# Layer 0: the product behind the MLP's norm takes six feature tiles beside the norm instead of twelve

## The chip, the cores and the metric

The kernel runs on one core of a Trainium2 chip. The metric is device time in microseconds (us) of one execution, as the median of several runs. A core has a matrix engine (TensorE, PE in the profile; its weight loads are listed apart as PEld), a vector engine (VectorE, DVE), a scalar engine (ScalarE, ACT), a general engine (GpSimd, POOL) and a queue engine (SyncE, SP) that here only issues DMA transfers. Each engine takes its instructions in the order in which the program lists them.

## The reference

Two layers over 256 tokens of 2048 features. Each layer normalises the residual `x`, scales and shifts it with values made from a conditioning vector, runs two groups of attention, adds the gated result, normalises again and runs a dense MLP:

```
mod = cond @ w_ada[l] + b_ada[l]
sh_a, sc_a, g_a, sh_m, sc_m, g_m = split(mod, 6)
...
h = _rmsnorm(x) * (1.0 + sc_m) + sh_m
y = square(relu(h @ w_mlp_in[l])) @ w_mlp_out[l]
x = x + g_m * y
```

`w_mlp_in` is 2048 x 8192. The change concerns the first quarter of its columns in layer 0 (2048 features, 16 tiles of 128 columns, called feature tiles here), the norm ahead of that product and the work in the same queues. All arithmetic is float32; products run on two parts of each operand (below).

## The kernel before, in words

Every product is made from two-part numbers. A weight matrix arrives as float32 in a tile `raw` (SyncE issues the DMA, L173); ACT rounds it to a first part `hi` (L154) and DVE takes the rest, `lo = raw - hi` (L157). Activations have the same two parts. A product is then hi x hi, hi x lo and lo x hi. Seven `raw` buffers and four each of `hi` and `lo` are there, so that weights are at most a few pieces ahead of the matmuls.

There are two ways to multiply one weight tile with the 256 tokens. In `mac` (L197, L200, L201) it takes three matmuls with 256 columns each, and all three land in one half of a bank of PSUM. In the wide form the two parts of the activation stand side by side as 512 columns: one matmul of 512 columns (L220 in `wides`, L287 in `wide_by_k`) makes both hi products, into the two halves of a bank, and one of 256 columns (L223, L284) adds the lo product. A wide tile needs a bank of its own, and the halves have to be added later (`joined`: a copy on ACT, L1440, and an addition on DVE, L1441).

`norm_then_by_k` makes the second norm of a layer and multiplies as it goes. It turns `x` by 128 features, and for each of eight steps p it makes two k tiles of `h` (two times 128 features): DVE scales (`ht`, L715), ACT adds the shift and rounds to the first part (L718), DVE makes the second part (L723). Then the weights of the two k tiles are prepared and multiplied into all open banks. In layer 0 it keeps 12 feature tiles in six banks, two a bank, by `by_k` and `mac`; each step p takes two pieces of weights of 128 x 1536. In layer 1 it keeps six feature tiles in six banks by `wide_by_k`, with one such piece a step. `first_block` then (layer 0) makes the relu and square of the 12 tiles, the other four tiles with `wides`, and the product with the first quarter of `w_mlp_out` (`rows`, L314 to L317).

Between all this runs the conditioning work. `mod` needs 192 pieces of `w_ada` of 1 MB: `ada_load` issues one DMA into a `raw` buffer, and `ada_sums` multiplies and sums it on DVE (L383), an instruction on 128 x 2048 elements. Two such sums give two columns of one group of `mod` (L395 or L397). How many are issued is set by a credit: each call of `weights` adds `self.rate`, and a piece is loaded for each full 1.0 (`more_ada`); its sum stands behind a later piece of weights on DVE. `ada_need` loads at once whatever the norm needs and lacks. The pieces of the shift and scale of layer 0's second norm are themselves among those that are still summed while that norm runs: step p reads columns 2p and 2p+1.

Of the kernel before, what the change touches and what calls it, by code (L numbers as in the profile page):

```python
# [94 lines left out]
WHOLE = 6  # L95


RATE_A0, RATE_V, RATE_A1, RATE_A2, RATE_K, RATE_K1, RATE_M0 = 1.1, 1.6, 0.6, 0.9, 0.6, 0.3, 1.0
RATE_M3 = 0.75
RATE_S, RATE_R, RATE_E = (0.1, 0.2), (0.8, 0.5), 0.3  # L100
RAWS = 7
# [3 lines left out]
class Trunk:  # L105
# [636 lines left out]
    def norm_then_by_k(self, l, sh, sc, src):  # L742

        nc = self.nc
        end = self.last_mm
        raws = [self.raw(src[0, b], 1536) for b in range(2 - l)]
        parts = [self.part(raws[0], i, 768)[0] for i in range(2)]
        r, rb = self.s("rms"), self.bank("pn")[:, 0]
        x = [self.turned(0, end)]
        self.behind(self.last_square, self.last_turn)  # L750
        root = [self.roots(r, t) for t in range(2)]
        self.spread_one(rb, r, 0, self.last_turned)
        x.append(self.turned(1, self.last_spread, True, self.last_x))
        self.behind(root[1][1], self.last_turn)
        x.append(self.turned(2, self.last_turned, False, root[1][0]))
        act = self.last_turn
        x.append(self.turned(3, self.last_turned, True, root[1][1]))
        x.append(self.turned(4, self.last_turned, False, act))
        act = self.last_turn
        late = [self.turn_in(i, self.last_turned) for i in (5,)]  # L760
        self.spread_one(rb, r, 1, self.last_turned)
        late += [self.turn_in(i, self.last_spread) for i in (6, 7)]
        h, gate, banks = [], None, None
        for p in range(8):
            k = 2 * p
            for g in (sh, sc):
                self.ada_need(l, g, k + 1)
            new, ins = self.modulated(x[p], rb, k, self.mod[l, sh], self.mod[l, sc], gate, act if p == 0 else None)
            gate = None
            h += new  # L770
            if p == 0:
                x += [self.turn_out(ps, False, self.last_h) for ps in late]
                banks = self.open_banks(6)
                gate = ins, self.last_turn
                for i in range(2, 2 * len(raws)):
                    w, ins = self.part(raws[i // 2], i % 2, 768, ins)
                    parts.append(w)
                blocks = [(parts[2 * b : 2 * b + 2], 768) for b in range(len(raws))]
            else:
                order = (self.last_h, ins) if p == 1 else None  # L780
                blocks = self.by_k_weights([src[p, b] for b in range(2 - l)], 6, False, order)
            if l == 0:
                self.by_k(banks, blocks, h, k, NK, 6, apart=p == 0)
            else:
                self.wide_by_k(banks, blocks, h, k, NK)
        return h, banks

    def first_norm_then_by_k(self, acc, src, n, fill, early):
# [96 lines left out]
    def layer(self, l, acc=None):  # L885
# [160 lines left out]

        self.quiet = False
        self.rate = RATE_K1 if l else RATE_K
        h, banks = self.norm_then_by_k(l, 3, 4, io["w_m0"] if l == 0 else io["w_m01"])
        self.kept = {}  # L1050
        if l == 0:
            self.first_block(h, banks)
# [6 lines left out]
    def first_block(self, h, banks):  # L1059

        io = self.io
        hid = []
        self.rate = RATE_M0
        for b in banks:
            hid += self.relu2(b)
        for m in range(12, NK, 2):
            ps = self.wides([io["w_m10"][m + j - 12] for j in range(2)], h)
            hid += self.relu2(self.joined(ps, self.t("sum")))
        left = []
        for c in range(4):  # L1070
            pss = self.rows(io["w_m2"][0, 0], hid, c)
            left.append(pss)
            if c == 1:
                self.keep_left(left)
            elif c > 1:
                self.keep_right(pss, c)

    def last_block(self, h):

        io = self.io  # L1080
        hid, acc = [], {}
        self.rate = RATE_M3
        self.gate(0, 5)
        steps = [lambda: self.read_kept(acc, (1, 2, 3)), lambda: self.read_kept(acc, (4, 5, 6, 7)),
                 lambda: self.add_halves(self.merged(acc))]
        for m in range(0, NK, 2):
            ps = self.wides([io["w_m10"][NK * 3 + m + j - 12] for j in range(2)], h)
            hid += self.relu2(self.joined(ps, self.t("sum")))
            if m > 4 and steps:
                steps.pop(0)()  # L1090
        for c in range(4):
            pss = self.rows(io["w_m2"][0, 3], hid, c, c == 3)
            self.updates(pss, c, True)
            if c == 0:
                self.read_kept(acc, [(t, c) for c in (2, 3) for t in range(2)])
            elif c == 1:
                for t, g in ((0, 2), (1, 2), (0, 3), (1, 3)):
                    self.add_rows(acc[t, g], t, g)
# [19 lines left out]
    def block_by_seven(self, l, fb, h, banks):  # L1118
# [8 lines left out]
        for m in range(plain, NK, 2):  # L1127
            both = self.t("sum")
            for j in range(2):
                src = io["w_m11"][NK * fb + m + j - 6] if l else io["w_m10"][NK * fb + m + j - 12]  # L1130
                ps = self.wides([src], h)[0]
                self.join(ps, both[:, j])
                if len(pairs) > 1:
                    pairs[-2][j]()
            r = self.relu(both)
            parts = self.split(r, "hid")
            hid += parts
            pairs.append(self.seven(io[f"w_ms{l}"][fb, m // 2], parts, r, sums, m == plain, m == NK - 2))
            if end and m == 2:
                self.gate(l, 5)  # L1140
# [508 lines left out]
def _kquarters(w, c=512, per=4):  # L1649
    k = w.shape[0] // P  # L1650
    return np.ascontiguousarray(w.reshape(k // per, per, P, c).transpose(0, 2, 1, 3)).reshape(k // per, P, per * c)
# [11 lines left out]
def _layout(i):  # L1663
    f = {k: np.asarray(v) for k, v in i.items()}
    a = {}
# [19 lines left out]
    for l in range(2):  # L1685
        w = f["w_in"][l]
        first = np.concatenate([w[:, 3072:3840], w[:, :768]], 1)
        if l == 0:
            a["w_a"] = np.stack([_kquarters(np.ascontiguousarray(first[:, 768 * j : 768 * j + 768]), 768, 2) for j in range(2)], 1)
        else:  # L1690
            a["w_a1"] = _kquarters(np.ascontiguousarray(first[:, :768]), 768, 2)[:, None]
            a["w_q1"] = _ktiles(np.ascontiguousarray(first[:, 768:]))
        keep["w_t"].append(_ktiles(np.ascontiguousarray(w[:, 1280:2048])))
        keep["w_d"].append(_kquarters(np.concatenate([w[:, 1024:1280], w[:, 768:1024]], 1)))
# [8 lines left out]
        w = np.concatenate([f["w_o"][l][1024:], f["w_o"][l][:1024]])  # L1703
        keep["w_o"].append(_kcols(w))
        w = f["w_mlp_in"][l]
        if l == 0:
            a["w_m0"] = np.stack([_kquarters(np.ascontiguousarray(w[:, 768 * j : 768 * j + 768]), 768, 2) for j in range(2)], 1)
        else:
            a["w_m01"] = _kquarters(np.ascontiguousarray(w[:, :768]), 768, 2)[:, None]
        a[f"w_m1{l}"] = _ktiles(np.ascontiguousarray(w[:, 1536 - 768 * l :]))  # L1710
        keep["w_m2"].append(np.stack([_kcols(f["w_mlp_out"][l][D * b : D * b + D]) for b in range(NFB)]))
    for l in range(2):
        a[f"w_ms{l}"] = np.stack([_kblocks(f["w_mlp_out"][l][D * b : D * b + D, :1024]) for b in range(NFB)])
# [21 lines left out]
```

## Time and profile before

| | us |
|---|---|
| median of 3 runs | 2141.35 (2141.03 to 2141.7) |
| the profiled execution | 2140.8 |
| its span in the profile | 2139.0 |
| first matmul of the product beside layer 0's second norm | 400.11 |
| first matmul of the four later tiles | 469.49 |
| the same two places in layer 1 (six tiles beside the norm) | 1441.09 and 1474.98 |

Times in the trace count from the start of the span. A row of the timeline gives the start of a group of equal instructions, the time from the start of the first to the end of the last, engine, line, operation, output and inputs, the shape and the count. Instructions of one engine overlap by their latency: of DVE's and ACT's rows the step from one start to the next is what the engine needs, and the last row's end is when the result is there. An entry in square brackets is idle time ahead of the row and what ended it.

### The profile page before, as it was taken

What the parts mean: (1) busy time and instruction counts of PE and PEld (TensorE: products, weight loads), DVE (VectorE), ACT (ScalarE), POOL (GpSimd) and SP (SyncE); (2) the same over time, 40 slices, a digit from 0 to 9 for tenths busy, and PEclk for the clock granted to TensorE, in tenths of its full rate; (3) what the DMA queues carried; (4) which work ended last, traced back from release to release, by engine and by line L of the source; (5) the groups of instructions that cost most, each with busy time, mean ns of one, the idle gap of its engine ahead of it and who ended that gap; (6) DMA issues with size and microseconds to landing.
All of it is one profiled execution on the core that took longest, in us unless ns stands there. A gap on an engine that the chain in (4) does not pass through costs nothing.

```text
span 2139.0 us, 29861 instructions
## 1 busy us (share of the span) xinstructions
PE 2112.4 (99%) x11363; PEld 1828.4 (85%) x11363; DVE 1805.1 (84%) x2453; ACT 1262.3 (59%) x1868; POOL 82.4 (4%) x121
## 2 busy tenths in 40 slices
PE   7999999999999999999999999999999999999998
PEld 6899888898888888888889998888888888888886
DVE  8889888989799888879977896789977985885898
ACT  6555663564466566645454576647755665674674
POOL 0000000000000100111000000000010010010010
PEclk9999999999999999999999999999999999999999
DMA  9999898789965965899968777877595687566664
GB/s 397 423 386 340 320 353 350 284 315 408 387 218 189 363 235 212 296 403 381 396 252 302 281 280 255 305 270 246 210 376 221 236 264 243 197 232 215 216 225 145
DMA packets 99264, 621.80 MB, mean 291 GB/s; under 512 B 11504, under 2 KB 11952, under 8 KB 32304
## 3 DMA queue, kind: packets, MB, share of 16 engines
q1 hardware_dynamic: 85536, 586.41, 72.4%
q0 software_dynamic: 12864, 32.28, 6.1%
q8 instruction: 89, 1.46, 0.3%
q10 hardware_dynamic: 720, 1.19, 0.2%
q14 instruction: 55, 0.45, 0.1%
HBM read 595.43 MB, written 21.27 MB: 288 GB/s over the span
## 4 chain that ended last, share of the span: by engine, by line
PE 94%; DVE 2%; DMA 2%; ACT 1%; issue 0%; SPq 0%; ACTq 0%; DVEq 0%
PE ps L220 20%; PE ps L223 10%; PE pr L314 9%; PE pr L315 9%; PE pr L317 9%; PE pp L1273 3%; PE pp L1275 3%; PE pp L1274 3%; PE pk L263 3%; DMA ada<-in_w_ada 2%; PE pk L197 2%; PE pk L201 2%; PE pk L200 2%; PE pk L287 2%; PE pv L299 2%; PE pv L301 2%
## 5 line engine op out<-in xcount | busy, mean ns | idle before, releaser
L154 ACT ACTIVATE hi<-raw 128x1024 fp32r<-128x1024 f32 (+2 forms) x714 | 713.0, 1010 | 499.6 <-PE pr L315 177.4
L157 DVE TENSOR_TENSOR lo<-raw,hi 128x1024 fp32r<-128x1024 f32 (+2 forms) x714 | 813.6, 1161 | 220.9 <-ACT hi L154 95.3
L383 DVE SCALAR_TENSOR_TENSOR ada<-ada,cond 128x2048 f32<-128x2048 f32 x192 | 438.7, 2287 | 13.4 <-DMA ada<-in_w_ada 12.4
L220 PE MATMUL ps<-h,hi 128*128 128x512 f32 x1856 | 441.0, 391 | 0.3 <-DVE sum L1441 0.2
L220 PEld LDWEIGHTS ps<-h,hi 128*128 128x128 f32 x1856 | 344.0, 188 | 75.5 <-DVE sum L1441 5.5
L314 PE MATMUL pr<-hi,hidh 128*128 128x512 f32 x640 | 249.1, 389 | 0.1
L315 PE MATMUL pr<-hi,hidl 128*128 128x512 f32 x640 | 249.0, 389 | 0.0
L223 PEld LDWEIGHTS ps<-h,lo 128*128 128x128 f32 x1856 | 236.4, 191 | 8.1
L223 PE MATMUL ps<-h,lo 128*128 128x256 f32 x1856 | 238.9, 283 | 0.0
L317 PE MATMUL pr<-lo,hidh 128*128 128x512 f32 x640 | 158.7, 389 | 0.0
L314 PEld LDWEIGHTS pr<-hi,hidh 128*128 128x128 f32 x640 | 120.2, 188 | 25.4 <-ACT hi L154 0.5
L317 PEld LDWEIGHTS pr<-lo,hidh 128*128 128x128 f32 x640 | 120.1, 188 | 24.9
L315 PEld LDWEIGHTS pr<-hi,hidl 128*128 128x128 f32 x640 | 120.1, 188 | 24.9
L157 DVE TENSOR_TENSOR lo<-comb,hi 128x1024 fp32r<-128x1024 f32 x90 | 109.9, 1221 | 6.4 <-ACT hi L154 3.4
L154 ACT ACTIVATE hi<-comb 128x1024 fp32r<-128x1024 f32 x90 | 94.7, 1053 | 17.2 <-PE pp L1275 12.2
L197 PE MATMUL pk<-h,hi 128*128 128x256 f32 x320 | 90.4, 285 | 0.2 <-ACT h L718 0.2
L201 PE MATMUL pk<-h,lo 128*128 128x256 f32 x320 | 90.5, 283 | 0.0
L200 PE MATMUL pk<-h,hi 128*128 128x256 f32 x320 | 90.5, 283 | 0.0
L1440 ACT ACTIVATE sum<-ps 128x256 f32<-128x256 f32 x110 | 41.7, 381 | 75.8 <-PE ps L223 74.8
L263 PE MATMUL pk<-hf,w 128*128 128x256 f32 x384 | 83.9, 379 | 0.0
L263 PEld LDWEIGHTS pk<-hf,w 128*128 128x128 f32 x384 | 72.6, 190 | 10.2 <-ACT hf L690 0.4
L1273 PE MATMUL pp<-hi,sh 128*128 128x512 f32 x180 | 70.2, 394 | 0.0
(292 smaller groups left out, 3431.9 us busy)
## 6 DMA issues: line engine op xcount, KB each, us to landing
ada<-in_w_ada SPq DMA_DIRECT2D x192, 1024.0 KB, 7.3
raw<-in_w_m SPq DMA_DIRECT2D x190, 1024.0 KB, 7.0
raw<-in_w_ms SPq DMA_DIRECT2D x48, 1024.0 KB, 5.4
raw<-in_w_o SPq DMA_DIRECT2D x32, 1024.0 KB, 6.3
raw<-in_w_m SPq DMA_DIRECT2D x24, 768.0 KB, 5.8
kept<-part POOLq DMA_DIRECT2D x69, 256.0 KB, 9.9
raw<-in_w_dv SPq DMA_DIRECT2D x16, 1024.0 KB, 5.8
raw<-in_w_t SPq DMA_DIRECT2D x12, 1024.0 KB, 5.3
```

The lines of the kernel that those rows point to most:

```text
L154: ins = self.nc.scalar.activation(hi, v, AF.Copy)
L157: ins = self.nc.vector.tensor_tensor(lo, v, hi.bitcast(F32), ALU.subtract)
L200: mm(ps, hi, x[1], start=False, stop=False, skip_group_check=shared)
L201: self.last_mac = mm(ps, lo, x[0], start=False, stop=last, skip_group_check=shared)
L220: mm(ps.rearrange("p a b -> p (a b)"), part(w, k, 0), x[2], start=k == 0, stop=False)
L223: mm(ps[:, 0], part(w, k, 1), x[0], start=False, stop=k == nk - 1)
L263: self.nc.tensor.matmul(ps, v, whole[k], start=first, stop=last, skip_group_check=True)
L314: mm(ps, xh[:, c], part(i, 0), start=kq == 0 and i == 0, stop=False)
L315: mm(ps, xl[:, c], part(i, 0), start=False, stop=False)
L317: self.last_mm = mm(ps, xh[:, c], part(i, 1), start=False, stop=kq == 3 and i == 3)
L383: ins = nc.vector.scalar_tensor_tensor(w, w, 1.0, self.cond, ALU.mult, ALU.mult, accum_out=acc[:, i : i + 1])
L1273: nc.tensor.matmul(ps, x[0], wh, start=first, stop=False)
```

## The change

Layer 0 now does what layer 1 does. `norm_then_by_k` takes six feature tiles in six banks with `wide_by_k`, and one piece of 128 x 1536 a step; `first_block` joins the six banks by pairs and makes ten later tiles, not four, with `wides`. The weights are laid out to suit. Two rates change: `RATE_K` (the calls in layer 0's second norm) from 0.6 to 1.0, and `RATE_M0` (`first_block`) from 1.0 to 0.85.

```diff
-RATE_A0, RATE_V, RATE_A1, RATE_A2, RATE_K, RATE_K1, RATE_M0 = 1.1, 1.6, 0.6, 0.9, 0.6, 0.3, 1.0
+RATE_A0, RATE_V, RATE_A1, RATE_A2, RATE_K, RATE_K1, RATE_M0 = 1.1, 1.6, 0.6, 0.9, 1.0, 0.3, 0.85
...
-        raws = [self.raw(src[0, b], 1536) for b in range(2 - l)]
+        raws = [self.raw(src[0], 1536)]
...
-                blocks = self.by_k_weights([src[p, b] for b in range(2 - l)], 6, False, order)
-            if l == 0:
-                self.by_k(banks, blocks, h, k, NK, 6, apart=p == 0)
-            else:
-                self.wide_by_k(banks, blocks, h, k, NK)
+                blocks = self.by_k_weights([src[p]], 6, False, order)
+            self.wide_by_k(banks, blocks, h, k, NK)
...
-        for b in banks:
-            hid += self.relu2(b)
-        for m in range(12, NK, 2):
-            ps = self.wides([io["w_m10"][m + j - 12] for j in range(2)], h)
+        plain = len(banks)
+        for m in range(0, plain, 2):
+            hid += self.relu2(self.joined(banks[m : m + 2], self.t("sum")))
+        for m in range(plain, NK, 2):
+            ps = self.wides([io["w_m10"][m + j - 6] for j in range(2)], h)
             hid += self.relu2(self.joined(ps, self.t("sum")))
```

The other lines of the diff only follow the new layout of the weights (indices, names and the arrays made on the host).

What this does to the order of the queues is seen at three places.

**Steps p = 2 to 4 of layer 0's second norm, on DVE.** `lo` is a piece of weights of one k tile, `ada` a conditioning sum, `ht` and `h` the activations; the number at the end of a name tells buffers apart. Before, there were two pieces of weights, four `lo`, to a step:

```order
L157 TENSOR_TENSOR lo_3725<-raw_3722,hi_3724 128x768
L157 TENSOR_TENSOR lo_3729<-raw_3722,hi_3728 128x768
L383 SCALAR_TENSOR_TENSOR ada_3438,macc_82<-ada_3438,cond 128x2048
L157 TENSOR_TENSOR lo_3739<-raw_3736,hi_3738 128x768
L397 TENSOR_TENSOR mod_81<-macc_82,vec 128x2
L157 TENSOR_TENSOR lo_3743<-raw_3736,hi_3742 128x768
L383 SCALAR_TENSOR_TENSOR ada_3734,macc_84<-ada_3734,cond 128x2048
L723 SCALAR_TENSOR_TENSOR h_3820<-ht_3819,mod_81,h_3820 128x256
L723 SCALAR_TENSOR_TENSOR h_3821<-ht_3819,mod_81,h_3821 128x256
```

After the change, from the weights of step 2 to those of step 4:

```order
L157 TENSOR_TENSOR lo_3714<-raw_3711,hi_3713 128x768
L157 TENSOR_TENSOR lo_3718<-raw_3711,hi_3717 128x768
L383 SCALAR_TENSOR_TENSOR ada_3676,macc_84<-ada_3676,cond 128x2048
L715 SCALAR_TENSOR_TENSOR ht_3748<-xT_3585,mod_83,pn_3553 128x256 x2
L157 TENSOR_TENSOR lo_3760<-raw_3757,hi_3759 128x768
L723 SCALAR_TENSOR_TENSOR h_3749<-ht_3748,mod_81,h_3749 128x256
L723 SCALAR_TENSOR_TENSOR h_3750<-ht_3748,mod_81,h_3750 128x256
L157 TENSOR_TENSOR lo_3764<-raw_3757,hi_3763 128x768
L383 SCALAR_TENSOR_TENSOR ada_3722,macc_84<-ada_3722,cond 128x2048
L715 SCALAR_TENSOR_TENSOR ht_3795<-xT_3592,mod_83,pn_3553 128x256
L395 SCALAR_TENSOR_TENSOR mod_83<-macc_84,vec 128x2
L715 SCALAR_TENSOR_TENSOR ht_3795<-xT_3592,mod_83,pn_3553 128x256
```

So one `ada` now stands in each step, ahead of that step's `ht`, where a step has half the `lo` and half the matmuls of before. On ACT, in the same steps after the change (step 3 has `h_3749` and `h_3750`; the four `hi` ahead of them belong to steps 3 and 4):

```order
L154 ACTIVATE hi_3759<-raw_3757 128x768
L154 ACTIVATE hi_3763<-raw_3757 128x768
L154 ACTIVATE hi_3806<-raw_3804 128x768
L154 ACTIVATE hi_3810<-raw_3804 128x768
L718 ACTIVATE h_3749<-ht_3748,mod_81 128x256
L718 ACTIVATE h_3750<-ht_3748,mod_81 128x256
```

**The last step, p = 7, on DVE.** Before, its two `h` stood apart, with one sum of another group between:

```order
L383 SCALAR_TENSOR_TENSOR ada_4165,macc_84<-ada_4165,cond 128x2048
L157 TENSOR_TENSOR lo_4265<-raw_4262,hi_4264 128x768
L395 SCALAR_TENSOR_TENSOR mod_83<-macc_84,vec 128x2
L715 SCALAR_TENSOR_TENSOR ht_4345<-xT_3625,mod_83,pn_3555 128x256
L157 TENSOR_TENSOR lo_4269<-raw_4262,hi_4268 128x768
L383 SCALAR_TENSOR_TENSOR ada_4260,macc_86<-ada_4260,cond 128x2048
L723 SCALAR_TENSOR_TENSOR h_4346<-ht_4345,mod_81,h_4346 128x256
```

After the change, from step 6's `h` to step 7's first:

```order
L723 SCALAR_TENSOR_TENSOR h_3889<-ht_3888,mod_81,h_3889 128x256
L723 SCALAR_TENSOR_TENSOR h_3890<-ht_3888,mod_81,h_3890 128x256
L157 TENSOR_TENSOR lo_3904<-raw_3897,hi_3903 128x768
L383 SCALAR_TENSOR_TENSOR ada_3862,macc_84<-ada_3862,cond 128x2048
L383 SCALAR_TENSOR_TENSOR ada_3908,macc_84<-ada_3908,cond 128x2048
L157 TENSOR_TENSOR lo_3948<-raw_3945,hi_3947 128x768
L395 SCALAR_TENSOR_TENSOR mod_83<-macc_84,vec 128x2
L157 TENSOR_TENSOR lo_3952<-raw_3945,hi_3951 128x768
L715 SCALAR_TENSOR_TENSOR ht_3936<-xT_3623,mod_83,pn_3553 128x256 x2
L157 TENSOR_TENSOR lo_4021<-raw_4018,hi_4020 128x1024
L723 SCALAR_TENSOR_TENSOR h_3937<-ht_3936,mod_81,h_3937 128x256
```

Two sums in a row now stand ahead of step 7. On PE the program after the change puts 14 matmuls of the first later tile between step 6 and step 7 (`ps_4017` is that tile's bank, `pk_3625` a bank of the norm's product); the last five of the 14 and what follows:

```order
L220 MATMUL ps_4017<-h_3797,hi_4024 128x512
L220 MATMUL ps_4017<-h_3842,hi_4024 128x512
L220 MATMUL ps_4017<-h_3843,hi_4024 128x512
L220 MATMUL ps_4017<-h_3889,hi_4024 128x512
L220 MATMUL ps_4017<-h_3890,hi_4024 128x512
L287 MATMUL pk_3625<-h_3937,hi_3947 128x512
```

**Steps 1 to 3 of layer 1's second norm, on DVE.** The code there is untouched, but the credit arrives with another remainder. Before:

```order
L383 SCALAR_TENSOR_TENSOR ada_13111,macc_98<-ada_13111,cond 128x2048
L723 SCALAR_TENSOR_TENSOR h_13374<-ht_13373,mod_93,h_13374 128x256
L397 TENSOR_TENSOR mod_97<-macc_98,vec 128x2
L723 SCALAR_TENSOR_TENSOR h_13375<-ht_13373,mod_93,h_13375 128x256
L157 TENSOR_TENSOR lo_13385<-raw_13382,hi_13384 128x768
L157 TENSOR_TENSOR lo_13389<-raw_13382,hi_13388 128x768
L715 SCALAR_TENSOR_TENSOR ht_13416<-xT_13258,mod_95,pn_13226 128x256 x2
```

After the change:

```order
L383 SCALAR_TENSOR_TENSOR ada_12935,macc_98<-ada_12935,cond 128x2048
L723 SCALAR_TENSOR_TENSOR h_13200<-ht_13199,mod_93,h_13200 128x256
L397 TENSOR_TENSOR mod_97<-macc_98,vec 128x2
L723 SCALAR_TENSOR_TENSOR h_13201<-ht_13199,mod_93,h_13201 128x256
L157 TENSOR_TENSOR lo_13211<-raw_13208,hi_13210 128x768
L157 TENSOR_TENSOR lo_13215<-raw_13208,hi_13214 128x768
L383 SCALAR_TENSOR_TENSOR ada_13173,macc_98<-ada_13173,cond 128x2048
L715 SCALAR_TENSOR_TENSOR ht_13243<-xT_13082,mod_95,pn_13050 128x256 x2
```

A second sum stands ahead of step 3 there; before, the second came between steps 5 and 6. In layer 1's first norm, the other way round, the second sum moves one step later.

More of the change, by code (lines that the diff above doesn't have):

```diff
@@ L1048, in layer @@
         self.rate = RATE_K1 if l else RATE_K
-        h, banks = self.norm_then_by_k(l, 3, 4, io["w_m0"] if l == 0 else io["w_m01"])
+        h, banks = self.norm_then_by_k(l, 3, 4, io[f"w_m0{l}"])
         self.kept = {}
@@ L1086, in last_block @@
         for m in range(0, NK, 2):
-            ps = self.wides([io["w_m10"][NK * 3 + m + j - 12] for j in range(2)], h)
+            ps = self.wides([io["w_m10"][NK * 3 + m + j - 6] for j in range(2)], h)
             hid += self.relu2(self.joined(ps, self.t("sum")))
@@ L1129, in block_by_seven @@
             for j in range(2):
-                src = io["w_m11"][NK * fb + m + j - 6] if l else io["w_m10"][NK * fb + m + j - 12]
+                src = io[f"w_m1{l}"][NK * fb + m + j - 6]
                 ps = self.wides([src], h)[0]
@@ L1690, in _layout @@
         else:
-            a["w_a1"] = _kquarters(np.ascontiguousarray(first[:, :768]), 768, 2)[:, None]
+            a["w_a1"] = _kquarters(np.ascontiguousarray(first[:, :768]), 768, 2)
             a["w_q1"] = _ktiles(np.ascontiguousarray(first[:, 768:]))
@@ L1705, in _layout @@
         w = f["w_mlp_in"][l]
[L1706 to L1710, printed above, removed]
+        a[f"w_m0{l}"] = _kquarters(np.ascontiguousarray(w[:, :768]), 768, 2)
+        a[f"w_m1{l}"] = _ktiles(np.ascontiguousarray(w[:, 768:]))
         keep["w_m2"].append(np.stack([_kcols(f["w_mlp_out"][l][D * b : D * b + D]) for b in range(NFB)]))
```

## The prediction

> **What bounds the kernel now.** I read the page first: the share of each engine, then the chain that ended last.
>
> ```profile
> span 2139.0 us, 29861 instructions
> PE 2112.4 (99%) x11363; PEld 1828.4 (85%) x11363; DVE 1805.1 (84%) x2453; ACT 1262.3 (59%) x1868; POOL 82.4 (4%) x121
> PE 94%; DVE 2%; DMA 2%; ACT 1%; issue 0%; SPq 0%; ACTq 0%; DVEq 0%
> ```
>
> The matmuls are 94% of the chain. Of PE's waits between 400 and 2100 us the longest line is this one (for whom, us in total, times, longest):
>
> ```profile
> PE pp L1273 <- ACT hi L154: 0.9, 1, 0.9
> PE pk L284 <- ACT h L718: 0.5, 2, 0.2
> ```
>
> So PE hardly waits there, and whatever PE gains or loses in one stage reaches the end almost whole. Next I asked for windows over the stage that changes, and over the same stage in layer 1, which already has the form that layer 0 gets.
>
> ```profile
> core 0: us, PE busy (x) PEld busy (x) DVE busy (x) ACT busy (x) POOL busy (x), PEclk, DMA share, GB/s
> 405.00:415.00 10.00, 10.00 (x85) 10.00 (x85) 10.00 (x14) 4.80 (x7) 0.00 (x0) 1.00 0.84 297
> 425.00:435.00 10.00, 10.00 (x86) 10.00 (x85) 9.97 (x14) 4.80 (x8) 0.00 (x0) 1.00 0.95 331
> 1450.00:1460.00 10.00, 10.00 (x58) 8.74 (x57) 10.00 (x19) 6.19 (x12) 0.00 (x0) 1.00 0.91 313
> ```
>
> The point is the fourth column: DVE is full in both stages, at a granted clock of 1.00. PE is served, but with nothing to spare.
>
> **PE's own work.** The timeline gives the pace of the two forms.
>
> ```profile
> 400.11 0.62 PE L197 MATMUL pk<-h,hi 128*128 128x256 f32 x3 [0.24 <-ACT h L718]
> 469.25 0.28 PE L200 MATMUL pk<-h,hi 128*128 128x256 f32 x1
> 469.37 0.28 PE L201 MATMUL pk<-h,lo 128*128 128x256 f32 x1
> 469.49 3.82 PE L220 MATMUL ps<-h,hi 128*128 128x512 f32 x16
> 1441.09 0.62 PE L284 MATMUL pk<-h,lo 128*128 128x256 f32 x3 [0.24 <-ACT h L718]
> 1449.78 1.55 PE L287 MATMUL pk<-h,hi 128*128 128x512 f32 x6
> 1451.17 0.88 PE L284 MATMUL pk<-h,lo 128*128 128x256 f32 x6
> 1453.98 1.55 PE L287 MATMUL pk<-h,hi 128*128 128x512 f32 x6
> 1474.98 3.82 PE L220 MATMUL ps<-h,hi 128*128 128x512 f32 x16
> 1478.64 2.08 PE L223 MATMUL ps<-h,lo 128*128 128x256 f32 x16
> 1480.55 3.82 PE L220 MATMUL ps<-h,hi 128*128 128x512 f32 x16
> ```
>
> Twelve tiles beside the norm take 469.49 - 400.11 = 69.38 us, 0.12 a matmul and 0.36 a tile and k tile. Six wide tiles take 1474.98 - 1441.09 = 33.89: a step (two k tiles) is 1453.98 - 1449.78 = 4.20, or 0.35 a tile and k tile. A later wide tile takes 1480.55 - 1474.98 = 5.57. So PE's work is 69.38 + 4 x 5.57 = 91.66 before and 33.89 + 10 x 5.57 = 89.59 after: **-2.1 us**, if nothing keeps it waiting.
>
> [...] The rows show 120 for 256 columns and 232 (1.39/6) for 512, and I keep 2.1.
>
> **DVE's queue beside the norm.** A step loses half its matmuls and half its `lo`, but each of the eight steps keeps its `ht` and `h`, and the seven sums (`ada`) that this norm itself needs must all come before step 7. I priced the new order from the same instructions in layer 1.
>
> ```profile
> 399.04 0.87 DVE L715 SCALAR_TENSOR_TENSOR ht<-xT,mod,pn 128x256 f32<-128x256 f32 x2
> 1440.01 0.87 DVE L715 SCALAR_TENSOR_TENSOR ht<-xT,mod,pn 128x256 f32<-128x256 f32 x2
> 1446.19 2.29 DVE L383 SCALAR_TENSOR_TENSOR ada<-ada,cond 128x2048 f32<-128x2048 f32 x1
> 1448.41 0.48 DVE L723 SCALAR_TENSOR_TENSOR h<-ht,mod,h 128x256 fp32r<-128x256 f32 x1
> 1448.81 0.15 DVE L397 TENSOR_TENSOR mod<-macc,vec 128x2 f32<-128x2 f32 x1
> 1448.88 0.48 DVE L723 SCALAR_TENSOR_TENSOR h<-ht,mod,h 128x256 fp32r<-128x256 f32 x1
> 1449.27 1.82 DVE L157 TENSOR_TENSOR lo<-raw,hi 128x768 fp32r<-128x768 f32 x2
> 1451.01 0.87 DVE L715 SCALAR_TENSOR_TENSOR ht<-xT,mod,pn 128x256 f32<-128x256 f32 x2
> 1451.79 0.95 DVE L157 TENSOR_TENSOR lo<-raw,hi 128x768 fp32r<-128x768 f32 x1
> 1452.66 0.88 DVE L723 SCALAR_TENSOR_TENSOR h<-ht,mod,h 128x256 fp32r<-128x256 f32 x2
> 1468.62 0.48 DVE L723 SCALAR_TENSOR_TENSOR h<-ht,mod,h 128x256 fp32r<-128x256 f32 x1
> 1470.28 2.38 DVE L157 TENSOR_TENSOR lo<-raw,hi 128x1024 fp32r<-128x1024 f32 x2
> ```
>
> From start to start: two `ht` 0.78, two `h` 0.79, a `lo` of 768 columns 0.87 and of 1024 about 1.15, a sum 2.22, a `mod` 0.07. Layer 0 starts its first `ht` at 399.04 and its first matmul at 400.11; layer 1 at 1440.01 and 1441.09. The two agree to 0.02 and their queues are equal up to the `lo` of step 2, so I put layer 0's new queue on layer 1's clock.
>
> Step 3: layer 1 starts its `ht` at 1451.01. There the new order has a sum first; `ht` starts at 1453.23, one `lo` later `h` starts at 1454.88 and is there at 1455.36. PE wants it at 1453.98: **1.4 late**. From step to step the new queue holds 0.78 + 0.79 + 2 x 0.87 + 2.22 = 5.53, and 5.60 with a `mod`, against PE's 4.20. Steps 4, 5 and 6 add 1.40, 1.33 and 1.40. From step 6's first `h` to step 7's there are two `h`, three `lo` of 768, two sums, a `mod`, two `ht` and a `lo` of 1024: 0.79 + 2.61 + 4.44 + 0.07 + 0.78 + 1.15 = 9.84. PE has step 6 (4.20) and the 14 matmuls drawn forward (14 x 3.66/16 = 3.20): 2.4 late. Sum: 1.4 + 1.4 + 1.3 + 1.4 + 2.4 = **+7.9 us** of waiting for DVE's `h`. While PE waits there nothing else is queued ahead on it; behind it DVE and ACT have the later tiles' weights, at 5.57 a tile with about 3 us of DVE plus a sum, so PE isn't kept there again.
>
> ACT makes a second chain of the same length. In the new order `h` of step n stands behind both `hi` of step n+1, and the second of these needs the buffer that PE frees with the second group of 512 columns of step n-1.
>
> ```profile
> 1451.37 0.85 ACT L154 ACTIVATE hi<-raw 128x768 fp32r<-128x768 f32 x1 [1.25 <-PE pk L287]
> 1452.12 0.89 ACT L718 ACTIVATE h<-ht,mod 128x256 fp32r<-128x256 f32 x2
> ```
>
> The first `hi` starts 0.20 after its group ended (1451.17). The second would start 2.10 + 1.39 + 0.20 = 3.69 after the step, `h`'s first part 0.75 later, 0.5 long, then 0.1 and DVE's 0.48: 5.5 to 5.6 a step again. So shorter sums alone would not shorten the wait.
>
> The joins: 12 more, each about 0.4 on ACT and on DVE, beside ten tiles of 5.57; the rest of the weights are the same bytes. I cost them and `RATE_M0` at nothing; if uncovered, the last join before `rows` would cost some 2 us. The ends for layer 0 are 0 and about 11 us of waits; I take 7.9, since all its terms are rows of the same instructions.
>
> **Layer 1's norms.** The second norm gets a sum ahead of step 3, as above: 1.4 late. Its third sum stands ahead of step 7: today's first `h` there starts at 1468.62, with 2.3 more it is there at 1471.4, and PE (1470.78, now 1.4 later) wants it at 1472.2. So **+1.4** (0 to 2). In the first norm the one wait today goes when the sum moves a step later, **-0.45** (0 to -0.45):
>
> ```profile
> 1122.02 1.67 PE L287 MATMUL pk<-h,hi 128*128 128x512 f32 x6 [0.45 <-DVE h L723]
> ```
>
> **Sum.** -2.1 + 7.9 + 1.4 - 0.45 = +6.8 us. The profiled execution took 2140.8 (its span 2139.0 and 1.8 around it): 2147.6. The median of the runs is 0.55 above that execution: **2148.2 us**.
>
> **Rivals.**
> - *The wait stays hidden (not slower).* Were DVE's `h` always ahead, only -2.1 and -0.45 remain: 2138.8. It turns on the sums per step: DVE has 3.31 us of other work in PE's 4.20, so 0.40 of a sum fits and one doesn't. For it speaks that layer 1 waits nowhere with two sums; against, that layer 0 has seven. 6%.
> - *Half of it.* The lead that DVE has at step 3 (0.84 in layer 1: 1453.14 against 1453.98) is larger in layer 0, or instructions run closer together: 4 us of waits, about 2144.4. 12%.
> - *Transfers become the bound.* A new step moves 0.79 + 1.05 MB in 5.6 us, 328 GB/s, what the stage carries today at a DMA share of 0.95. A buffer freed by step n's `lo` is wanted as step n+3's weights about 6.0 us after the issue:
>
> ```profile
> raw<-in_w_m SPq DMA_DIRECT2D x10, 768.0 KB, 6.0
> ```
>
>   That is the median landing. If landings take 7.5, each of two turns of the seven buffers adds 1.5: 2151. 8%.
> - *Weight loads are the bound (faster).* PEld is 10.00 of 10 in layer 0's stage and 8.74 in layer 1's. If loads set the pace at 0.12 each, two instead of three save 192 x 0.12 = 23 us: 2118. Against it, layer 1 shows 0.35 for two loads and not 0.24. 3%. [...]
>
> **How the numbers follow.** Forecast 71%, with the four rivals 6, 12, 8 and 3. A measurement of this kernel can tell about 0.2%, 4.3 us, from no change. Slower by more: 71 + 8, and a hair of the half case, 0.80. Within: the hidden case and most of the half, 0.17. Faster: 0.03. The range 2143.5 to 2151.5 leaves out the hidden case, the loads, and the ends of the half and the transfer cases, some 18%.
>
> **What would show it.** In the new profile, PE's waits: about 8 us for DVE's `h` at L287 in layer 0, in five pieces ahead of steps 3 to 7, the last the longest; a piece of 1.4 in layer 1's second norm and none in its first. The stretch from 400 to the first `rows` would grow from 91.7 to about 97.5. If the waits end on the DMA of `raw` or on ACT's `hi`, the transfers decide. If PE has none and the stretch is 89.6, the queue count is wrong. If the total is off with these waits as said, the loss or gain is in a stage that I took as unchanged, where the sums have also moved.

## The result and the profile after

| | us |
|---|---|
| before, median of 6 runs beside the changed kernel | 2141.68 (2141.03 to 2143.5) |
| after, median of 6 runs | 2150.22 (2148.95 to 2150.71) |
| ratio | 1.0038, 95% interval 1.0027 to 1.0049 |
| the profiled execution after, and its span | 2150.71, 2148.9 |

The change makes the kernel slower by 8.5 us; the forecast was 2148.2, and the measured median lies inside the forecast's range of 2143.5 to 2151.5. The profiled executions differ by more, 2150.71 - 2140.8 = 9.9 us. The page of the profile after, its span and busy times:

```profile
span 2148.9 us, 29476 instructions
PE 2110.8 (98%) x11171; PEld 1819.8 (85%) x11171; DVE 1806.5 (84%) x2461; ACT 1266.5 (59%) x1876; POOL 82.3 (4%) x121
```

PE has 1.6 us less work and ends 9.9 us later: what was won in matmuls is lost in waits. PE's waits between 400 and 2140 us (for whom, us in total, times, longest) name them:

```profile
PE pk L287 <- DVE h L723: 8.3, 6, 2.1
PE pp L1271 <- ACT hi L154: 3.7, 4, 0.9
...
PE pp L1272 <- DVE lo L157: 0.5, 1, 0.5
```

Five of the six waits for `h` are in layer 0's second norm and one is in layer 1's. PE's timeline of the kernel after shows them, with the rows that bound the stages:

```profile
401.12 0.61 PE L284 MATMUL pk<-h,lo 128*128 128x256 f32 x3 [0.24 <-ACT h L718]
413.29 0.87 PE L284 MATMUL pk<-h,lo 128*128 128x256 f32 x6
415.43 1.66 PE L287 MATMUL pk<-h,hi 128*128 128x512 f32 x6 [1.27 <-DVE h L723]
416.93 0.88 PE L284 MATMUL pk<-h,lo 128*128 128x256 f32 x6
417.64 1.55 PE L287 MATMUL pk<-h,hi 128*128 128x512 f32 x6
419.03 0.87 PE L284 MATMUL pk<-h,lo 128*128 128x256 f32 x6
421.09 1.66 PE L287 MATMUL pk<-h,hi 128*128 128x512 f32 x6 [1.20 <-DVE h L723]
...
436.74 3.36 PE L220 MATMUL ps<-h,hi 128*128 128x512 f32 x14
442.25 1.66 PE L287 MATMUL pk<-h,hi 128*128 128x512 f32 x6 [2.15 <-DVE h L723]
...
498.93 0.40 PE L314 MATMUL pr<-hi,hidh 128*128 128x512 f32 x1
...
1461.57 1.66 PE L287 MATMUL pk<-h,hi 128*128 128x512 f32 x6 [1.28 <-DVE h L723]
```

A step that doesn't wait puts its next group 0.71 after the start of an L284 row (416.93 to 417.64). So the group at 415.43 is 415.43 - 414.00 = 1.43 late, the one at 421.09 is 1.35 late, and the last, 3.20 after 436.74, is 2.31 late. The bracket shows some 0.16 less each time, since the row ahead ends that much behind the place where the next group was due (416.93 + 0.88 = 417.81, against 417.64), and the first group after a wait takes 0.11 longer (416.93 - 415.43 = 1.50 in place of 1.39).

Windows of the kernel after, over the stretches that were shown for the kernel before (columns: busy PE, PEld, DVE, ACT, POOL, then granted clock, share of DMA, GB/s):

```profile
405.00:415.00 10.00, 9.16 (x53) 7.87 (x51) 10.00 (x15) 6.38 (x11) 0.00 (x0) 1.00 0.75 263
425.00:435.00 10.00, 7.61 (x43) 6.37 (x42) 9.95 (x15) 4.89 (x8) 0.00 (x0) 1.00 0.98 359
1450.00:1460.00 10.00, 10.00 (x58) 8.72 (x57) 9.87 (x15) 6.40 (x10) 0.00 (x0) 1.00 0.63 213
```

DVE was full before and is full now; PE has fallen from 10.00 to 7.61. One step on DVE's timeline shows of what it is full:

```profile
414.90 0.87 DVE L723 SCALAR_TENSOR_TENSOR h<-ht,mod,h 128x256 fp32r<-128x256 f32 x2
415.69 0.95 DVE L157 TENSOR_TENSOR lo<-raw,hi 128x768 fp32r<-128x768 f32 x1
416.56 2.28 DVE L383 SCALAR_TENSOR_TENSOR ada<-ada,cond 128x2048 f32<-128x2048 f32 x1
418.77 0.47 DVE L715 SCALAR_TENSOR_TENSOR ht<-xT,mod,pn 128x256 f32<-128x256 f32 x1
419.17 0.15 DVE L395 SCALAR_TENSOR_TENSOR mod<-macc,vec 128x2 f32<-128x2 f32 x1
419.24 0.47 DVE L715 SCALAR_TENSOR_TENSOR ht<-xT,mod,pn 128x256 f32<-128x256 f32 x1
419.63 0.95 DVE L157 TENSOR_TENSOR lo<-raw,hi 128x768 fp32r<-128x768 f32 x1
420.55 0.88 DVE L723 SCALAR_TENSOR_TENSOR h<-ht,mod,h 128x256 fp32r<-128x256 f32 x2
```

From `h` to `h` DVE takes 420.55 - 414.90 = 5.65 us, against PE's 4.20. It has no gap there but one of 0.05 ahead of the last row (420.55 - 419.63 = 0.92, where the first `lo` of these rows takes 416.56 - 415.69 = 0.87); the section on the prediction says what held it. Cut by stage, with the rows of before at the two places not shown so far,

```profile
491.94 0.40 PE L314 MATMUL pr<-hi,hidh 128*128 128x512 f32 x1
1104.32 0.62 PE L284 MATMUL pk<-h,lo 128*128 128x256 f32 x3 [0.24 <-ACT h L718]
```

and those of after

```profile
1111.66 0.63 PE L284 MATMUL pk<-h,lo 128*128 128x256 f32 x3 [0.24 <-ACT h L718]
1447.26 0.62 PE L284 MATMUL pk<-h,lo 128*128 128x256 f32 x3 [0.24 <-ACT h L718]
1482.66 3.82 PE L220 MATMUL ps<-h,hi 128*128 128x512 f32 x16
```

the 9.9 us of the spans fall apart like this:

| stage | before | after | change | forecast |
|---|---|---|---|---|
| to the first matmul beside layer 0's second norm | 400.11 | 401.12 | +1.0 | 0 |
| from there to the first `rows` (L314) | 91.83 | 97.81 | +6.0 | +5.8 |
| to layer 1's first norm | 612.38 | 612.73 | +0.35 | 0 |
| to layer 1's second norm | 336.77 | 335.60 | -1.2 | -0.45 |
| six tiles beside it | 33.89 | 35.40 | +1.5 | +1.4 |
| to the end | 664.02 | 666.24 | +2.2 | 0 |

### The profile page after: what moved, and what is told of

Read it like the earlier page. It is cut to its first block, busy times and chain, and to the rows that moved or that the text cites. A ratio compares the mean times of both kernels' runs of the same rounds, so it can differ in the third digit from the quotient of the medians.

```text
span 2148.9 us, 29476 instructions
## 1 busy us (share of the span) xinstructions
PE 2110.8 (98%) x11171; PEld 1819.8 (85%) x11171; DVE 1806.5 (84%) x2461; ACT 1266.5 (59%) x1876; POOL 82.3 (4%) x121
## 3 DMA queue, kind: packets, MB, share of 16 engines
q8 instruction: 87, 1.43, 0.2%
## 4 chain that ended last, share of the span: by engine, by line
PE 76%; DVE 2%; ACT 1%; DMA 0%; issue 0%; DVEq 0%; ACTq 0%
PE ps L220 19%; PE ps L223 10%; PE pr L317 8%; PE pr L314 8%; PE pr L315 8%; PE pp L1271 3%; PE pp L1272 3%; PE pp L1273 3%; PE pk L287 2%; PE pk L284 1%; DVE lo L157 1%; PE pv L299 1%; PE pv L300 1%; PE pv L301 1%; PE ps L200 1%; PE ps L201 1%
## 5 line engine op out<-in xcount | busy, mean ns | idle before, releaser
L220 PE MATMUL ps<-h,hi 128*128 128x512 f32 x1952 | 463.1, 391 | 0.2 <-DVE sum L1439 0.2
L220 PEld LDWEIGHTS ps<-h,hi 128*128 128x128 f32 x1952 | 361.6, 188 | 78.2 <-DVE sum L1439 4.8
L223 PEld LDWEIGHTS ps<-h,lo 128*128 128x128 f32 x1952 | 248.4, 191 | 8.5 <-DVE lo L157 0.2
L223 PE MATMUL ps<-h,lo 128*128 128x256 f32 x1952 | 251.0, 283 | 0.0
L314 PE MATMUL pr<-hi,hidh 128*128 128x512 f32 x640 | 249.2, 389 | 0.1
L314 PEld LDWEIGHTS pr<-hi,hidh 128*128 128x128 f32 x640 | 120.1, 188 | 25.4 <-ACT hi L154 0.5
L287 PE MATMUL pk<-h,hi 128*128 128x512 f32 x288 | 75.3, 397 | 8.3 <-DVE h L723 8.3
L1446 ACT ACTIVATE relu<-sum 128x512 f32<-128x512 f32 x64 | 40.4, 631 | 55.8 <-DVE sum L1439 55.8
L1272 PE MATMUL pp<-lo,sh 128*128 128x512 f32 x180 | 69.9, 391 | 0.0
L1273 PE MATMUL pp<-hi,sl 128*128 128x512 f32 x180 | 69.3, 390 | 0.0
```

What stands on the lines that cost most here:

```text
L220: mm(ps.rearrange("p a b -> p (a b)"), part(w, k, 0), x[2], start=k == 0, stop=False)
L223: mm(ps[:, 0], part(w, k, 1), x[0], start=False, stop=k == nk - 1)
L287: ins = mm(ps, part(j, 0), both, start=False, stop=False, skip_group_check=True)
L314: mm(ps, xh[:, c], part(i, 0), start=kq == 0 and i == 0, stop=False)
L1272: nc.tensor.matmul(ps, x[0], wl, start=False, stop=False)
L1273: nc.tensor.matmul(ps, x[1], wh, start=False, stop=last)
```

## The experiments

Twelve kernels ran, each beside the kernel before. In the quoted expectations "the theory of the prediction" is that the sums in DVE's queue and, as a second chain, the order on ACT make the waits; rival A takes DVE's queue alone, rival B the transfers. "Stretch" is the second line of the table. After the change the lines behind some 1050 stand two lower than before (L1271 was L1273); those of edited kernels are up to six higher again.

**Short sums.** What each sum costs on DVE is taken away: in layer 0's second norm it reads 64 of its 2048 columns and leaves the rest out. The bytes stay:

```diff
+            n = self.cut
...
-                w, w, 1.0, self.cond, ALU.mult, ALU.mult, accum_out=acc[:, i : i + 1]
+                w[:, :n], w[:, :n], 1.0, self.cond[:, :n], ALU.mult, ALU.mult, accum_out=acc[:, i : i + 1]
...
+        self.cut = D if l else 64
         h, banks = self.norm_then_by_k(l, 3, 4, io[f"w_m0{l}"])
+        self.cut = D
```

> The changed kernel, but in layer 0's second norm the conditioning sums read 64 of their 2048 columns (the rest of these sums is left out; all bytes are still loaded). Ahead of TensorE's steps VectorE's queue shrinks by some 2.2 us of 5.6 a step; ScalarE's queue still has the high parts of step n+1 ahead of h of step n. Theory of the prediction (two chains of the same length): the waits for h go down little, from 7.0 to some 4 to 6 us, and the stretch from the first matmul behind the norm to the first row product from 97.8 to some 95 to 97. Rival A (VectorE's queue alone): waits under 0.5 us, stretch 89.6 to 90.5. Rival B (transfers set the pace): the waits stay at 6 to 7 us, the last one of 2.1 too.

2141.92 us in one run, beside 2141.51 before. PE's waits from 395 to 500 us, and a window:

```profile
PE ps L221 <- ACT hi L155: 0.7, 1, 0.7
PE pk L285 <- ACT h L720: 0.2, 1, 0.2
```
```profile
425.00:435.00 10.00, 10.00 (x59) 8.80 (x59) 4.52 (x7) 4.05 (x8) 0.00 (x0) 1.00 1.02 428
```

No wait for DVE's `h` is left. DVE is down to 4.52 of 10, while the transfers run at 428 GB/s and keep up: rival B falls. The stretch is 491.25 - 400.53 = 90.72, or 90.0 without the 0.71 that a later tile waits for its `hi`. On the second chain this run says less than was meant. The instructions of ACT did not keep their order: with shorter sums the scheduler put `h` of step 3 (`h_3749`, `h_3750`) ahead of the `hi` of step 4,

```
L155 ACTIVATE hi_3759<-raw_3757 128x768
L155 ACTIVATE hi_3763<-raw_3757 128x768
L720 ACTIVATE h_3749<-ht_3748,mod_81 128x256
L720 ACTIVATE h_3750<-ht_3748,mod_81 128x256
L155 ACTIVATE hi_3806<-raw_3804 128x768
```

where the changed kernel has the four `hi` first. The run shortened DVE's queue and took ACT's chain away with it.

**`h` first.** The other part alone, with the sums whole. The edit goes a little further than the expectation says: `order` holds the parts of step n's own weights behind step n's `h`, and so those of step n+1 as well.

```diff
-                order = (self.last_h, ins) if p == 1 else None
+                order = (self.last_h, ins) if p == 1 or (l == 0 and sh == 3) else None
```

> The changed kernel, but in layer 0's second norm the high and low parts of step n+1 are queued behind h of step n on ScalarE and VectorE; nothing is left out, VectorE has the same work a step (5.5 to 5.7 us). Theory of the prediction (two chains) and rival A (VectorE alone): the waits stay, 6.5 to 8 us, stretch 97 to 98.5. A rival in which ScalarE's order alone makes the wait: waits under 1 us, stretch 89.6 to 90.5. Rival B (transfers): no change.

2150.88 us in one run. The waits stay and change their name; PE's waits from 395 to 500 us and the rows of the longest:

```profile
PE pk L287 <- ACT hi L154: 7.8, 3, 4.5
```
```profile
439.15 2.93 PE L287 MATMUL pk<-h,hi 128*128 128x512 f32 x6 [4.49 <-ACT hi L154]
442.73 1.54 PE L287 MATMUL pk<-h,hi 128*128 128x512 f32 x6
```

The wait is named for `hi` because the edit put the step's `hi` behind its `h`, and `h` behind `ht` and the sum on DVE. With ACT's old order out of the way PE waits as long as before; that the sums make this wait, and not the new order, is shown by the next run, which has the same order with short sums. The stretch is 500.38 - 400.04 = 100.34, 1.8 above what was expected; the group behind the longest wait took 2.93 in place of 1.66.

**Both.** The two diffs together.

> Both edits together: sums of 64 of 2048 columns in layer 0's second norm (the rest of them is left out), and h of step n ahead of the parts of step n+1. Theory of the prediction: only with both does the wait go, to under 0.5 us, stretch 89.6 to 90.5. Rival A: the same as with the short sums alone. Rival B (transfers): waits stay at 6 to 7 us, now named as waits for the parts.

2143.5 us in one run; the stretch is 492.67 - 401.94 = 90.73, that of the short sums to 0.01, and the waits are the same two lines. The order adds nothing to the short sums. And this run differs from the one before it in the length of the sums alone: 100.34 - 90.73 = 9.6 us of the stretch are theirs, the slow group behind the longest wait included, so DVE's queue is enough to make the wait.

**Low parts on GpSimd.** An attempt to relieve DVE with all of the work kept; in layer 0's second norm every second low part of the weights goes to GpSimd:

```diff
+        if self.pool_lo and i:
+            self.nc.gpsimd.tensor_tensor(lo, v, hi.bitcast(F32), ALU.subtract)
+            return (hi, lo), ins
         ins = self.nc.vector.tensor_tensor(lo, v, hi.bitcast(F32), ALU.subtract)
```

> The changed kernel, but in layer 0's second norm the low part of every second weight half is subtracted on GpSimd, which is idle there; nothing is left out. VectorE's step falls from 5.6 to some 4.65 us (one low part of 0.95 less), against TensorE's 4.2. Theory of the prediction: each of the four steps waits 0.4 to 1.4 instead of 1.2 (the upper end if ScalarE's chain holds it), 2 to 5 us in all with the last one. Rival A (VectorE alone): 0.45 a step, 1.5 to 2.5 us in all. If GpSimd takes over 4 us for a part, or slows VectorE beside it, the wait turns into one for the low part on GpSimd and is longer than 7 us.

2156.12 us in one run: worse. DVE's groups by shape from 402 to 446 us (count, busy us, mean ns), first of the kernel after, then of this one, and GpSimd's:

```profile
L383 DVE SCALAR_TENSOR_TENSOR ada<-ada,cond 128x2048 f32<-128x2048 f32 x8 | 18.2, 2285 | 0.0
```
```profile
L387 DVE SCALAR_TENSOR_TENSOR ada<-ada,cond 128x2048 f32<-128x2048 f32 x7 | 22.5, 3222 | 0.0
```
```profile
L159 POOL TENSOR_TENSOR lo<-raw,hi 128x768 fp32r<-128x768 f32 x8 | 19.2, 2404 | 115.1 <-PE pr L321 87.0 <-ACT hi L155 21.2 <-PE pk L288 6.9
```

GpSimd needs 2.4 us for what DVE does in 0.95, and a sum that runs beside it grows from 2.28 to as much as 3.94 (rows in the last section). The waits for `h` are 8.8 us, and 1.3 more for a low part; the last of the three expectations holds in its size, by way of the slowed DVE, though the wait is still mostly one for `h`.

**The later rate.** Is the rest of the loss the credit?

```diff
-... 0.3, 0.85
+... 0.3, 0.823077
```

> The changed kernel with the rate of sums behind the norm set so that the sums of the rest of the program fall where they fell before the change (0.823 in place of 0.85). Layer 0's norm keeps its work: waits for h of 6.5 to 7.5 us there in every theory. What differs behind it: if the later differences (1.3 us of waits in layer 1's second norm, 1.8 us at two waits for high parts near 600 us, 2.2 us at the end) come from sums that fell elsewhere, they go and 0.45 us of layer 1's first norm comes back, 2145.5 to 2148.5; if they come from the later bytes and buffers, the time stays at 2149.5 to 2151.

2149.37 us (2147.06 to 2153.07, 6 runs), ratio 1.0037 (1.0025 to 1.0049). The total, 0.9 above the first expectation, can't be told from 2150.22; the trace tells more. From the first `rows` to the end it takes 2147.6 - 501.25 = 1646.35; after 2148.9 - 498.93 = 1649.97, before 2139.0 - 491.94 = 1647.06. The waits behind the norm are those of before again (0.9 at `pp`, 0.4 in layer 1's first norm), so the credit that arrived with another remainder is a part of the changed kernel's loss: 3.6 us by these two traces. One trace of each is little for such a number. The four kernels above, which have the change's rates behind the norm, take 1648.7 to 1649.0 for the same part, and the kernel with one sum in a gap (below), which has the later rate, 1647.95: some 2 us on average. In the total they hardly show. In the profiled execution 0.8 went ahead of the norm (401.89 - 401.12), and more in it, where the last wait is followed by matmuls at a slower pace:

```profile
440.00:460.00 20.00, 17.86 (x92) 15.27 (x91) 18.74 (x25) 12.83 (x22) 0.00 (x0) 0.91 0.97 354
```
```profile
443.01 2.69 PE L287 MATMUL pk<-h,hi 128*128 128x512 f32 x6 [2.14 <-DVE h L723]
445.50 1.43 PE L284 MATMUL pk<-h,lo 128*128 128x256 f32 x6
446.76 1.55 PE L287 MATMUL pk<-h,hi 128*128 128x512 f32 x6
```

446.76 - 443.01 = 3.75 for the two groups that take 2.20 behind the same wait after the change (442.25 to 444.45). That is 1.55 us, and the stretch is 99.36 in place of 97.81. The clock granted from 444 to 446 us is 0.50.

**Sums brought forward.** All is computed; rates decide how many pieces are loaded and summed before the norm (`RATE_V` in the product with `w_dv`, a new rate with `w_o`, `RATE_A0` from the attention's first products on). `RATE_K` and `RATE_M0` are set so that the rest falls as before the change.

```diff
three sums (e6):             RATE_V 2.2, RATE_K 0.4, RATE_M0 0.8
three sums, two places (e7): RATE_V 1.9, with w_o 1.4, RATE_K 0.3, RATE_M0 0.7577
one sum (e8):                RATE_V 1.9, with w_o 1.6, RATE_K 0.0, RATE_M0 0.7308
from the attention (e9):     RATE_A0 1.4, with w_o 1.1, RATE_K 0.4, RATE_M0 0.834616
```

> The changed kernel with three of the seven conditioning sums left in layer 0's second norm, four brought forward to the product with w_dv, and the sums behind the norm where they were before the change; all is computed. VectorE's queue alone as the cause (it has 3.4 us a step without a sum, 5.6 with one, against TensorE's 4.2): a step with a sum is late only by what the steps without one don't make up, waits of 0 to 1.5 us in the norm, 2141 to 2144 in all. If the loads brought forward are late for the products ahead of the norm (four loads of 1 MB, some 2.8 us each at 370 GB/s), new waits of up to 11 us stand there, 2146 to 2156.

> As the last one, but the sums brought forward go half to the product with w_dv and half to that with w_o, and the norm's three stand as two together and one. VectorE alone: the two together (4.5 us) make one wait of 1 to 2.5 us; 2142 to 2145. If the loads brought forward are late: new waits of up to 11 us between 330 and 400 us, 2146 to 2156.

> As the last one, with six sums brought forward and one left in the norm. VectorE alone: no waits for h in the norm, 2140 to 2143. If the loads brought forward are late: new waits of up to 17 us between 230 and 400 us, 2146 to 2160.

> Three sums left in the norm as in the run with four brought forward to the product with w_dv, but these four are spread over the products ahead of it (from some 130 us on), where the transfers have 8 to 21 per cent of their time free in four of six slices of 20 us, and VectorE 0.1 to 4.7 us a slice. If what the forward loads cost is the seven buffers of the weights just ahead of w_dv and w_o, it is cheaper here: waits ahead of the norm of 0 to 4 us more than in the changed kernel, norm waits under 1 us, 2142 to 2146. If any sum brought forward costs its load and its 2.3 us wherever it stands: 9 to 14 us ahead of the norm, 2150 to 2156.

The credit runs on into the next group of `mod`, so that the sums added ahead of the norm are more than those taken out of it.

| | us (runs) | ratio, interval | first matmul of the norm | stretch | sums left in the norm | sums more ahead of it |
|---|---|---|---|---|---|---|
| after | 2150.22 (6) | 1.0038 (1.0027 to 1.0049) | 401.12 | 97.81 | 7 | 0 |
| e6 | 2151.9 (4) | 1.0048 (1.0031 to 1.0065) | 413.90 | 90.28 | 3 | 5 |
| e7 | 2160.61 (4) | 1.0085 (1.007 to 1.01) | 421.66 | 91.07 | 3 | 6 |
| e8 | 2164.62 (4) | 1.0107 (1.0092 to 1.0122) | 425.95 | 89.43 | 1 | 9 |
| e9 | 2149.36 (4) | 1.0038 (1.0023 to 1.0053) | 410.21 | 90.97 | 3 | 4 |

In the norm they do what DVE's queue says. With three single sums the waits for `h` are 0.4 us (e6) or 1.3 (e9, above the 1 us expected), with two together and one 1.4 (e7), with one sum none, and then the stretch is 89.43, the bare matmuls. But each sum more costs 2.3 to 3.4 us ahead of the norm ((410.21 - 401.12)/4 and (421.66 - 401.12)/6), more than the 2.2 us that it takes on DVE. PE's waits up to 395 us in e6, where the kernel after has none for `pv`, and a window of each from 260 us, the kernel after first:

```profile
PE pv L299 <- ACT hi L154: 5.7, 2, 3.7
```
```profile
260.00:280.00 20.00, 20.00 (x94) 16.75 (x94) 18.28 (x29) 11.66 (x23) 0.00 (x0) 1.00 0.93 340
```
```profile
260.00:280.00 20.00, 16.23 (x62) 12.51 (x61) 15.77 (x25) 8.34 (x19) 0.00 (x0) 0.83 0.73 270
```

There the weights of `w_dv` come later (`pv` waits for their `hi`) though the transfers are not full, 270 GB/s; I read it as the added pieces' turns of the seven `raw` buffers, but whether buffers, transfers or DVE's own queue set the price was not told apart. The granted clock there is 0.83 in place of 1.00, and PE was busy 0.26 us a matmul (16.23/62) in place of 0.21 (20.00/94): a part of the price is a slower pace of the matmuls beside the waits. Spread further ahead (e9) a sum costs the least, 2.3, but no less than it saves: the waits are smaller and more, the longest this one, and the time lies between the two expectations. e7 and e8 are above the upper one.

```profile
PE pss L197 <- ACT hi L154: 2.6, 1, 2.6
```

**One sum into a gap.** After its last `lo` for `w_o` DVE waits 2.1 us for PE. The sum whose piece has landed by then goes there; no load moves. It has the later rate too.

```diff
             w = [self.weights(src[c, kq]) for kq in (2, 3)]
+            if self.early:
+                self.ada_sums(self.last_part)
```

> The changed kernel with the later rate, and one sum, whose bytes have landed, moved from the norm into the 2.1 us in which VectorE waits for TensorE at the last product with w_o (389.9 to 392.0); no load moves. VectorE's queue alone as the cause: the waits in the norm fall by one sum, from 7.0 to some 4.7 us, and 0.2 to 1.1 us are lost ahead of the norm; 1.2 to 2.1 us below the run with the later rate, 2147 to 2148.5. If the waits in the norm stay at 7.0, the sums there are not what sets them.

2146.71 us (2145.53 to 2147.74, 10 runs), ratio 1.0023 (1.0013 to 1.0032): 2.7 below the later rate alone, where 1.2 to 2.1 were expected, and the best of the changed form, yet slower than before. PE's waits from 395 to 500 us:

```profile
PE pk L288 <- DVE h L726: 5.2, 4, 2.1
```

One wait of five is gone and 1.8 us of 7.0 (2.3 were expected), and the stretch is 497.35 - 401.63 = 95.72, 2.1 less than after, for one sum of 2.2 less. Here the last wait, 2.09, was not followed by slow matmuls (1.66 for six).

**The form with the rates of before.**

```diff
-... 0.9, 1.0, 0.3, 0.85
+... 0.9, 0.6, 0.3, 1.0
```

> The changed form with the two rates of before (0.6 in the norm, 1.0 behind it): the form alone. Seven sums stand in the norm as in the changed kernel, but four of them together ahead of h of the last step, three single. VectorE's queue alone as the cause: the waits are its work less TensorE's and so the same total, fewer early ones and one of 4 to 6 us at the end, 7 to 9 us in all (more if the four loads that go with them land late), 2150 to 2155. If the rates, not the form, made the loss: 2139 to 2143.

2152.9 us (2151.64 to 2153.51, 4 runs), ratio 1.0047 (1.0032 to 1.0062). Four sums stand together ahead of step 7, and the waits lump with them:

```profile
441.63 2.93 PE L287 MATMUL pk<-h,hi 128*128 128x512 f32 x6 [4.90 <-DVE h L723]
```

The total of the waits for `h` is 6.6, near the 7.0 of the even spread and a little under the 7 to 9 expected, and the time is in the first expectation's range. So the form makes the loss; the two rates of the change soften it.

**The kernel before with a sum in the gap.** The same edit as in e10, on the kernel before.

> The kernel before with one sum moved from the norm into the gap of VectorE ahead of it, as in the run of one sum into the gap. VectorE's queue is no bound in the norm there (no wait for h in the kernel before), so nothing is gained: 2141 to 2143, 0 to 1.1 us lost ahead of the norm. If the gain of that run came from elsewhere than the norm's waits (an earlier buffer, say), it shows here too: 2138.5 to 2140.

2142.55 us (2141.14 to 2143.91, 10 runs), ratio 1.0000 (0.9990 to 1.0009), as expected. Where DVE's queue isn't late, moving a sum out of it gains nothing. None of the twelve kernels was faster than before.

## Why the prediction was right

- **PE's own work, -2.1.** The stretch with no wait in it was forecast at 89.59 and came to 89.43 (e8), from 91.83: 91.83 - 89.43 = 2.4. The pace rests on rows of layer 1 (0.12 us a matmul of 256 columns and 1.39/6 = 0.232 one of 512), and it held.
- **DVE's queue, +7.9.** The mechanism held: five pieces, the last the longest. The late starts are 1.43 + 3 x 1.35 + 2.31 = 7.8 where 1.4, 1.4, 1.3, 1.4 and 2.4 were forecast; the waits of the trace show 7.0 of it for the reason given above. Not in the sum were the slower first groups, 5 x 0.11. Taken out by shorter sums (e1) the waits go, and by one sum at a time (e10, e6, e8) they shrink with it.
- **The second chain on ACT.** It is there, and as long as was said. Rows of the kernel after around step 5, ACT first; PE's second group of 512 columns in step 4 ended at 423.30 + 1.55 = 424.85:

```profile
424.93 0.85 ACT L154 ACTIVATE hi<-raw 128x768 fp32r<-128x768 f32 x1 [1.25 <-DVE ht L715]
425.69 0.89 ACT L718 ACTIVATE h<-ht,mod 128x256 fp32r<-128x256 f32 x2
```
```profile
425.21 0.95 DVE L157 TENSOR_TENSOR lo<-raw,hi 128x768 fp32r<-128x768 f32 x1
426.21 0.88 DVE L723 SCALAR_TENSOR_TENSOR h<-ht,mod,h 128x256 fp32r<-128x256 f32 x2
```

  The bracket names `ht`; but at step 3 the same `hi` starts at 413.49, ahead of the end of its `ht` (413.25 + 0.47 = 413.72), and 0.04 after the end of PE's group (411.90 + 1.55 = 413.45), so the buffer that PE frees is what it needs. DVE could go on 0.87 after the start of its `lo`, at 426.08, but starts `h` at 426.21, when ACT's first `h` (some 0.5 long) is there. So ACT's chain ends last at step 5, by 0.13 us, and by 0.05 and 0.07 at steps 4 and 6; at steps 3 and 7 it is DVE's queue. That is why PE's steps are 5.66 to 5.68 apart whether or not a `mod` stands in them. What failed is the sentence drawn from it: "So shorter sums alone would not shorten the wait". In e1 they removed it. It took the order of the changed kernel for fixed, and in e1 the scheduler's order changed with the length of the sums. The sums are enough for the wait without this order (e2 against e3). Whether ACT's order, held fixed, would keep PE waiting with short sums stays open: it was not tried.
- **`RATE_M0` at nothing.** The term that was mis-sized. The remainder of the credit moves the sums of the whole rest of the kernel. Forecast were +1.4 and -0.45 in layer 1's norms, and both are there (1.28 of waiting, stage +1.5; no wait in the first norm). Not forecast were waits in the later blocks of the MLP (`pp`), 3.7 + 0.5 in place of 0.9. From the first `rows` to the end the kernel after takes 1649.97 - 1647.06 = 2.9 us more than the kernel before, against the 0.95 that were counted, and the later rate takes some 2 us of such a loss back (3.6 in e5's trace). The joins did cost nothing that can be seen: they lie in the stretch, which without waits is 89.43 where 89.59 were forecast.
- **The start.** 1.0 us of the 9.9 arose ahead of the change. Windows of the first 20 us, before and after:

```profile
0.00:20.00 20.00, 10.02 (x47) 8.96 (x48) 12.67 (x28) 13.00 (x24) 0.87 (x8) 1.00 0.91 354
```
```profile
0.00:20.00 20.00, 9.26 (x44) 8.45 (x45) 12.77 (x28) 13.10 (x24) 0.87 (x8) 0.78 0.92 354
```

  The clock was granted at 0.78 in place of 1.00. It isn't the change: the kernel before with a sum in the gap starts at 0.76, and the form with the rates of before, at 1.00, has its first matmul of the norm at 400.23. The first 20 us are not all of it: e5 has 1.00 there, but 0.84 from 20 to 40 us, and its first matmul of the norm comes at 401.89.
- **The rivals.** The hidden wait and half of it are out by the waits themselves. Transfers are out by e1. Weight loads as the bound are out: PEld fell to 6.37 of 10 (425 to 435 us) and the kernel became slower, and with no wait the stretch shrank by 2.4, not 23.
- **The total.** By the spans 9.9 - 6.8 = 3.1 us were not in the sum: 1.0 at the start, 0.2 in the stretch and 1.9 behind it. The mechanism of the main term was right; that the total came inside the range with these left out is owed to the range's width.

## What to carry to other kernels

When a change shortens a step of the bounding engine, count again, per step, what the other engines do a fixed number of times: here the matmuls and low parts of a step were halved, but not the two `ht`, two `h` and one sum, and DVE went from hidden to late by 1.4 us a step. Work moved out of such a place is only gained where an idle gap takes it (e10, 2.1 us of the stretch for one sum); moved with its loads into the products ahead it cost 2.3 to 3.4 us a sum to save 2.2. Where side work is issued by a running count, compare its remainder behind the edit: here it was worth some 2 us far away from it, 3.6 in one pair of traces.

## What the runs showed of the hardware

- **In e2, e5 and e11 a pause of TensorE was followed by some 3 us at half the pace**, so that the wait cost more than its length. Six matmuls of 512 columns took 2.93 us behind waits of 4.49 (e2) and 4.90 (e11), 2.69 behind 2.14 (e5), but 1.66 behind 2.15 (after). The granted clock goes with it: 0.50 from 439 to 442 us in e2 and from 444 to 446 in e5, 1.00 from 442 to 445 in the kernel after. So a wait of 2.14 us (e5) was followed by it, and waits of 2.15 (after) and 2.09 (e10) weren't; what decides was not shown. Nor was it shown whether this also spreads the runs of one kernel (2147.06 to 2153.07 in e5), since only one run of each has a trace.
- **In e4 a sum on VectorE stood nearly still beside a low part on GpSimd.** Four of the seven sums in e4's norm took 3.92 to 3.94 us in place of 2.28, and each of the four started while a low part was under way on GpSimd. The first of them:

```profile
404.57 1.88 POOL L159 TENSOR_TENSOR lo<-raw,hi 128x768 fp32r<-128x768 f32 x1 [8.97 <-ACT hi L155]
```
```profile
404.67 3.94 DVE L387 SCALAR_TENSOR_TENSOR ada<-ada,cond 128x2048 f32<-128x2048 f32 x1
```

  It lost 1.66 of the 1.88. The profile's spans on GpSimd are rough. Why the sum stands still was not shown.
